# A transformer layer's second output projection in seven products of quarters, with sums made by accumulating transfers

## The chip, the core and the metric

The kernel runs on one core of a Trainium2 chip. A core has five engines with a queue each, which work in order and wait for one another through semaphores: TensorE (PE in the profile; PEld is its weight load), VectorE (DVE), ScalarE (ACT), GpSimd (POOL) and SyncE (SP). Transfers between on-chip memory and the large memory (DRAM) are issued from the queues of SP, ACT or POOL. The metric is the time of one execution on the device, in microseconds; lower is better. The time before is 1794.62 us, the median of three runs from 1794.32 to 1796.17.

## The reference

One decoder layer for 1024 tokens of width 1024, in float32. The part around the change:

```python
y_a = _sliding_window_attention(qa, ka, va, sinks) @ w_oa          # first output projection
y_b = _gated_deltanet(dq, dk, dv, z, b_raw, a_raw, ...) @ w_ob     # second output projection
mixed = (jax.nn.sigmoid(g_a) * y_a + jax.nn.sigmoid(g_b) * y_b) @ w_out
x = _layer_norm(ALPHA * x + (1.0 + gt1) * mixed, ln1_g, ln1_b)
```

Before it stand the input projection `u @ w_in`, which gives queries, keys, values, the gates `g_a`, `g_b` and the inputs of the DeltaNet heads, the attention itself and the recurrence of the eight heads. After it comes a squared-ReLU MLP of width 4096 and a second layer norm. `w_oa`, `w_ob` and `w_out` are 1024 x 1024.

## The kernel before

Activations are kept with the features on the 128 partitions and the tokens along the row. Every matmul operand is split into a high part, rounded by ScalarE (`A.activation` with a copy), and a low part, the rest, by VectorE (`split_s`, L206). A product of a 128x128 block of weights with 512 tokens is then three matmuls of 128x128 by 128x512: high by high, high by low, low by high (L248, L1608). 1024 features by 1024 features by 1024 tokens, done plainly, are 8 output blocks x 8 blocks of the sum x 2 halves of the tokens x 3 = 384 matmuls.

A product of two matrices, cut into quarters, can also be had from seven products of quarters (or of sums of quarters) instead of eight, with more additions. Before the change the first output projection (L1591 to L1619) and the MLP are done so: 7 products x 4 output pairs x 12 matmuls (4 blocks of the sum x 3) = 336 matmuls. The second output projection is plain: eight units of `stream_unit` (L238, L1635) with 48 matmuls each.

Order of work. The program for PE, VectorE and ScalarE is written out in order (`manual_schedule`). A counter, `count[0]`, goes up by one with every large matmul, and `at(p, f, ...)` (L189) puts the work of `f` in front of the matmul with number p. These positions decide an order and not a time: an engine still runs each instruction as soon as its operands are there, and waits in its queue if they aren't. SP and POOL get their transfers in an order that a scheduler makes from the same calls. The stages, with the names of their first positions:

- the gates, queries and keys of the attention, beside the attention of 64 slots of 16 positions (`slot(s)`, L954) and a triangular solve on VectorE. POOL adds score blocks here (`join`, L876) and masks probabilities (`mask`, L915)
- from `Q0`: the heads' inputs, beside the recurrence of the eight heads, 120 positions each (`PER`, L1002; head h begins at R0 + 120 h). Each step of the recurrence goes through PE, VectorE and ScalarE in turn (`hd_a`, `hd_b`, `hd_c`, L1265 to L1304). Extra work of VectorE and ScalarE is placed into free windows of this chain (`window`, L1006). At a head's end `hd_out` (L1330) turns its output, half of the tokens at a time, multiplies it by its gate in the tile `sz` (L1338) and stores `sz` to `og_d` (L1343, on POOL; L1341 for head 7, on SP). `sz` has one buffer: the next head's gate is loaded into it (L1170) when the store has read it
- from `OA`: the first output projection. Quarters `11`, `T2`, `T3`, `T4` of the attention's output are sums that VectorE makes on chip (`ts_step`, L1401; `q_part`, L1430); `21`, `T1`, `22` are loaded from DRAM into tiles `or` (`q_load`, L1421) and split (`q_split`). The sums of the weights are made by VectorE (`o_sum`, L1457). Four accumulators per output block are read while TensorE goes on: `o_part` (L1562, ScalarE) copies an accumulator into a tile `t` or `t0`, and the next product adds to the same accumulator 12 positions later; `o_full` (L1567, VectorE) adds a second accumulator to that tile and stores the block to `ta_d`
- position OA + 336: the second output projection, whose operands `og_load`/`og_split` (L1503) bring in from `og_d`. Its outputs are multiplied by the sigmoid of `g_b`, and `y_a` times the sigmoid of `g_a` is added (`y_load`, `yb_done`, L1574 to L1633), then split for the next stage
- from `E0`: the product with `w_out`, then the MLP

On-chip memory is handed from stage to stage in pools. At position OA + 26 (`CLOSE`, L1500) the heads' pools `pc` and `pce` end, and `big2` and `p2` (tiles `or` and `t`) are opened in the same memory (`open_p2`, L1514). `yo` (tiles `t0`) lives on.

Of the kernel before, what the change touches and what calls it, by code (L numbers as in the profile page):

```python
# [34 lines left out]
def hybrid_layer_kernel(ctx: ExitStack, tc: tile.TileContext,  # L35
# [39 lines left out]
    og_d = dram.tile([KT, P, S], F32, name="og_d")  # L75
# [76 lines left out]
    later = [in_cols(w_ob, f * P) for f in range(KT)]  # L152
# [816 lines left out]

    makers = {"g": gate_done, "k": k_done, "q": q_done}  # L970
# [359 lines left out]
    def hd_out(h, half):  # L1330
# [6 lines left out]
        def put():  # L1337
            V.scalar_tensor_tensor(out=d["sz"][:, halves[half]], in0=tp, scalar=normw, in1=d["sz"][:, halves[half]],  # L1338
                                   op0=ALU.mult, op1=ALU.mult)
            if h == 7:  # L1340
                nc.sync.dma_start(out=og_d[h, :, halves[half]], in_=d["sz"][:, halves[half]])  # L1341
            elif half == 1:
                nc.gpsimd.dma_start(out=og_d[h], in_=d["sz"])  # L1343
# [49 lines left out]
    def ts_load(k):  # L1393
        tags = (((pce, "qT", 3), (pce, "qT", 3)), ((pc, "Re", 1), (pce, "pad", 1)), ((pc, "kT", 2), (pc, "kd", 2)),
                ((pc, "E", 2), (pc, "vr", 2)))[k]
# [5 lines left out]
    def ts_step(k, n):  # L1401
        (r11, r12), (r21, r22) = [[t[:, halves[u]] for u in range(2)] for t in late[k]]
        sub(V, *((r12, r12, r11), (r22, r22, r12), (r21, r21, r22), (r12, r22, r11))[n])
# [37 lines left out]
    wraw, wop, opn = {}, {}, [0]  # L1441

    def o_load(i, pair):
        for j in range(2):
            t = (wp.tile([P, KT, P], F32, tag="wr", name="owr", bufs=2) if pair % 2 == 0 else
                 gpool.tile([P, S], F32, tag="gate", name="owg").rearrange("p (k c) -> p k c", k=KT))
            nc.sync.dma_start(out=t, in_=in_cols(w_oa, (pair + 4 * j) * P)[0])
            wraw[pair, j] = t[:, 0:4, :], t[:, 4:8, :]

    def o_op(i, which):  # L1450
        (f1l, f1h), (f2l, f2h) = wraw[i, 0], wraw[i, 1]
        src = {"a0": f1l, "a4": f1h, "g0": f1l, "g4": f1h, "b0": f2l, "b4": f2h, "d": f2h}[which]
        t = wop[i, which] = wp.tile([P, 2, 4, P], F32R, tag=("wh", "wl")[opn[0] % 2], name="wo")
        opn[0] += 1
        split_s(t[:, 0], t[:, 1], src, 5)

    def o_sum(i, what):  # L1457
        (f1l, f1h), (f2l, f2h) = wraw[i, 0], wraw[i, 1]
        if what == "b":
            add_(V, f2l, f2l, f2h)  # L1460
        elif what == "g0":
            sub(V, f1l, f2l, f1l)
        elif what == "g4":
            sub(V, f1h, f1h, f1l)
        elif what == "G4":
            add_(V, f1h, f1h, f1l)
            sub(V, f1h, f1h, f2l)
        else:
            sub(V, f2h, f2h, f1l)

    at(L0 - 56, o_load, 0, 0)
    at(L0 - 50, o_load, 0, 1)
    OPS = [(-76, 0, "a0"), (-70, 1, "a0"), (-64, 0, "+b"), (-61, 0, "+g0"), (-58, 1, "+b"), (-55, 1, "+g0"),
# [7 lines left out]
    for p, i, what in OPS:  # L1481
        at(OA + p, *((o_sum, i, what[1:]) if what[0] == "+" else (o_op, i, what)))
    for pair in (2, 3):
        at(OA + 97, o_load, 1, pair)

    REST = [(n, j) for n in ("21", "T1", "22") for j in range(2)]
    RSPLIT = (54, 60, 66, 86, 104, 112)

# [12 lines left out]
    oh, ol, ograw = [None] * KT, [None] * KT, {}  # L1501

    def og_load(k):  # L1503
        ograw[k] = p2.tile([P, S], F32, tag="or", name="or", bufs=3)
        nc.sync.dma_start(out=ograw[k], in_=og_d[k])

    def og_split(k):
        oh[k] = big2.tile([P, S], F32R, tag=f"h{k}", name=f"oh{k}")
        ol[k] = big2.tile([P, S], F32R, tag=f"l{k}", name=f"ol{k}")
        for half in range(2):  # L1510
            s_ = halves[half]
            after(4 * half, split_s, oh[k][:, s_], ol[k][:, s_], ograw[k][:, s_])
# [16 lines left out]
    OGK = (6, 7, 0, 1, 2, 3, 4, 5)  # L1529
    OGS = (180, 188, 208, 216, 224, 232, 246, 256)  # L1530
    for n, k in enumerate(OGK):
        at(OA + (150, 152, 154)[n] if n < 3 else OA + OGS[n - 3] + 6, og_load, k)
        at(OA + OGS[n], og_split, k)

# [10 lines left out]
    at(OA + 250, lambda: (wseq.extend(later), w_more()))  # L1545
    for p in (270, 291):
        at(OA + p, w_go)
        at(OA + p + 8, w_more)
# [10 lines left out]
    def o_put(i, c):  # L1559
        nc.gpsimd.dma_start(out=ta_d[i + 4 * (c // 2), :, halves[c % 2]], in_=ot[i, c])  # L1560

    def o_part(i, c, pt, last=False):  # L1562
        A.activation(out=o_tile(i, c), in_=pt, func=AF.Copy)
        if last:
            o_put(i, c)
# [779 lines left out]
```

## Time and profile before

The profile shows one execution. The chip's own time of that execution was 1793.83 us; its span from the first instruction to the last is 1792.1 us, so 1.7 us lie outside the span. It is 0.8 us below the median of the three runs.

| what | value |
|---|---|
| median of three runs | 1794.62 us (1794.32 to 1796.17) |
| profiled execution, its own time | 1793.83 us |
| its span | 1792.1 us |
| granted TensorE clock, mean | 0.999 |
| first output projection, first to last matmul start | 913.1 to 989.6 us |
| second output projection, the same | 989.8 to 1076.7 us |
| bytes moved by transfers | 350.32 MB |

How to read it: the page gives each engine's busy time and its share of the span. Matmuls are pipelined, so the duration in a matmul's row is longer than the distance to the next one's start, and a busy PE isn't PE at its peak. A row of a timeline begins with the start and the duration in us; what stands in square brackets is how long the engine was idle before it and who released it. A row of the waits reads: who waited, for whom, us in total, times, longest. Weights and other tiles go by the program's names (`or`, `t`, `sz`, `qh`), and L1563 is a line of the kernel.

### The profile page before, as it was taken

To read this page: it belongs to the slowest core of one execution; us is meant where nothing else is said; L and a number is where in the kernel's file an instruction comes from. 1 tells how busy PE (TensorE), PEld (TensorE's weight loads), DVE (VectorE), ACT (ScalarE), POOL (GpSimd) and SP (SyncE) were. 2 spreads that over 40 slices of the span, in tenths; PEclk is the share of its full clock that TensorE was granted. 3 is DMA by queue.
4 is the path that set the end of the run, shared out by engine and by line. 5 is a ranking of instruction groups with operands and counts; after the bars stand their busy time and mean duration, and the time that the engine had idled before them with its cause. 6 is when DMAs were issued, how large, how long until landed. Compare 5 with 4: busy or idle time off the path is not lost.

```text
span 1792.1 us, 26317 instructions
## 1 busy us (share of the span) xinstructions
PE 1778.8 (99%) x9134; PEld 1499.3 (84%) x9134; DVE 1305.3 (73%) x2411; ACT 1034.0 (58%) x2363; POOL 326.8 (18%) x478
## 2 busy tenths in 40 slices
PE   9999999999999999999999999999999999999998
PEld 6988888888888888888888888888888888888887
DVE  7689588888855576766687555888777766676697
ACT  4789578887874565655575432475555545434341
POOL 0334234544331011110002200002122210000000
PEclk9999999999999999999999999999999999999999
DMA  9656722232256566665657634369888889665671
GB/s 331 184 198 217 206 80 90 70 104 74 74 210 198 152 173 177 174 189 173 231 161 269 209 124 165 129 193 325 301 276 270 284 294 383 239 200 181 207 258 47
DMA packets 254295, 350.32 MB, mean 195 GB/s; under 512 B 26345, under 2 KB 158130, under 8 KB 253906
## 3 DMA queue, kind: packets, MB, share of 16 engines
q1 hardware_dynamic: 212146, 220.78, 38.5%
q0 software_dynamic: 31488, 106.85, 17.6%
q10 hardware_dynamic: 10528, 21.00, 3.2%
q8 instruction: 72, 1.18, 0.3%
q14 instruction: 61, 0.50, 0.1%
HBM read 238.74 MB, written 107.75 MB: 193 GB/s over the span
## 4 chain that ended last, share of the span: by engine, by line
PE 92%; DVE 3%; ACT 2%; DMA 1%; issue 0%; ACTq 0%; SPq 0%; DVEq 0%
PE mm L250 36%; PE mm L2206 8%; PE mm L2266 7%; PE a L2266 4%; PE b L2206 4%; PE b L2266 4%; PE a L2206 3%; PE mm L1611 2%; PE c L2266 2%; PE c L933 2%; PE mm L1835 1%; PE b L1611 1%; PE mm L178 1%; PE mm L180 1%; PE mm L179 1%; PE a L859 1%
## 5 line engine op out<-in xcount | busy, mean ns | idle before, releaser
L250 PE MATMUL mm<-uh,wh 128*128 128x512 f32 x800 | 319.6, 400 | 0.0
L250 PE MATMUL mm<-uh,wl 128*128 128x512 f32 x800 | 319.3, 399 | 0.0
L250 PE MATMUL mm<-ul,wh 128*128 128x512 f32 x800 | 318.8, 398 | 0.0
L208 DVE TENSOR_TENSOR sp<-sraw,sp 128x1024 fp32r<-128x1024 f32 x112 | 132.8, 1219 | 75.7 <-ACT sp L207 75.6
L207 ACT ACTIVATE sp<-sraw 128x1024 fp32r<-128x1024 f32 x112 | 112.7, 1053 | 120.7 <-PE b L2266 75.4
L250 PEld LDWEIGHTS mm<-uh,wh 128*128 128x128 f32 x800 | 150.7, 188 | 26.2
L250 PEld LDWEIGHTS mm<-ul,wh 128*128 128x128 f32 x800 | 150.8, 188 | 26.1
L250 PEld LDWEIGHTS mm<-uh,wl 128*128 128x128 f32 x800 | 150.8, 188 | 26.1
L2266 PE MATMUL mm<-sp 128*128 128x512 f32 x528 | 135.9, 389 | 0.0
L2266 PEld LDWEIGHTS mm<-sp 128*128 128x128 f32 x528 | 98.8, 188 | 20.3
L2266 PE MATMUL a<-sp 128*128 128x512 f32 x336 | 92.3, 389 | 0.0
L1282 ACT ACTIVATE vn<-a,brk 128x128 f32<-128x128 f32 x64 | 23.6, 369 | 111.0 <-PE a L1280 111.0
L866 DVE CUSTOM_DVE_ANT_0 nscore<-a,amask,nsink 128x256 f32<-128x256 f32 (+1 forms) x128 | 54.4, 462 | 44.3 <-PE a L859 44.1
L2266 PE MATMUL b<-sp 128*128 128x512 f32 (+1 forms) x336 | 79.7, 374 | 0.0
L877 POOL TENSOR_TENSOR sm<-sm 128x256 f32<-128x256 f32 x56 | 58.1, 1038 | 109.6 <-ACT sm L873 81.7
L225 DVE TENSOR_TENSOR wl<-wr,wh 128x1024 fp32r<-128x1024 f32 x56 | 72.6, 1297 | 7.0 <-ACT wh L221 6.7
L2266 PEld LDWEIGHTS a<-sp 128*128 128x128 f32 x336 | 63.1, 188 | 13.1
L2266 PEld LDWEIGHTS b<-sp 128*128 128x128 f32 x336 | 60.3, 188 | 11.2
L208 DVE TENSOR_TENSOR wl<-fraw,wh 128x1024 fp32r<-128x1024 f32 x43 | 52.5, 1221 | 16.5 <-ACT wh L207 16.5
L207 ACT ACTIVATE wh<-fraw 128x1024 fp32r<-128x1024 f32 x43 | 45.0, 1056 | 32.0 <-PE b L2206 27.0
L873 ACT ACTIVATE sm<-nscore,stat 128x257 f32<-128x257 f32 (+1 forms) x128 | 62.0, 487 | 0.4 <-DVE stat L866 0.2
L221 ACT ACTIVATE wh<-wr 128x1024 fp32r<-128x1024 f32 x56 | 59.0, 1054 | 0.7 <-PE mm L179 0.7
(567 smaller groups left out, 4733.4 us busy)
## 6 DMA issues: line engine op xcount, KB each, us to landing
wr<-in_w_in_dram SPq DMA_DIRECT2D x60, 512.0 KB, 3.6
sraw<-hf_d SPq DMA_DIRECT2D x54, 512.0 KB, 4.1
adaw<-in_w_ada_dram SPq DMA_DIRECT2D x83, 256.0 KB, 5.1
fraw<-in_w_ff_dram SPq DMA_DIRECT2D x32, 512.0 KB, 5.4
sraw<-wt_d SPq DMA_DIRECT2D x32, 512.0 KB, 4.3
hf_d<-t ACTq DMA_DIRECT2D x48, 256.0 KB, 4.6
wt_d<-wx POOLq DMA_DIRECT2D x48, 256.0 KB, 3.1
sraw<-in_w_ff_dram SPq DMA_DIRECT2D x22, 512.0 KB, 5.5
```

The source lines that it names most:

```text
L207: A.activation(out=hi, in_=src, func=AF.Copy)
L208: after(lag, lambda: V.tensor_tensor(out=lo, in0=src, in1=hi.bitcast(F32), op=ALU.subtract))
L221: A.activation(out=hl[0], in_=raw, func=AF.Copy)
L225: V.tensor_tensor(out=hl[1], in0=raw, in1=hl[0].bitcast(F32), op=ALU.subtract)
L250: T.matmul(ts[half], lhsT=w[:, k, :], rhs=xx[k][:, sl], start=k == 0 and m == 0, stop=k == KT - 1 and m == 2)
L866: V.tensor_tensor_reduce(out=ns[:, i, 1:1 + W], in0=sc[:, i * 2 * P:i * 2 * P + W], in1=amask[:, mo:mo + W], scale=-1.0, scalar=nsink[:, 2 ...
L873: A.activation(out=sm[:, i, 0:1 + W], in_=ns[:, i, 0:1 + W], func=AF.Exp, scale=-1.0, bias=st[:, i:i + 1], accum_out=st[:, 2 + i:3 + i])
L877: G.tensor_tensor(out=sm[:, :, 1 + P:1 + 2 * P], in0=sm[:, :, 1:1 + P], in1=sm[:, :, 1 + P:1 + 2 * P], op=ALU.add)
L933: T.matmul(av[:, 0:256], lhsT=vt[:, b, :], rhs=p_[:, m, :], start=p_ is full and m == 0, stop=p_ is prods[-1][1] and m == 1)
L1611: T.matmul(pt, lhsT=t[:, lw, k, :], rhs=r[:, k % 2, :], start=begin and k == 0 and x_ == 0, stop=k == 3 and x_ == 2, skip_group_check=True)
L2206: T.matmul(pt, lhsT=a[:, kk, :], rhs=b[k], start=begin and k == 0 and x_ == 0, stop=k == 3 and x_ == 2, skip_group_check=True)
L2266: T.matmul(to, lhsT=a[:, f, t * P:(t + 1) * P], rhs=b[:, f, lo:up], start=(begin or own) and s % NS == 0 and f == 0 and x_ == 0, stop=s % ...
```

## The change

The second output projection is also made of seven products of quarters, 336 matmuls; both projections now run through one loop over `(stage, i, m)`, with pairs of output blocks sharing a weight tile of 128 x 4 x 256. What that needs:

- The sums of quarters of both weight matrices are made in DRAM (`ws_d`) during the attention stage: 16 plain copies of 512 KB from SP (`ws_put`) and 28 transfers of 512 KB from POOL that add to what is there (`ws_add`, `accum_op`). The sums on VectorE (`o_sum`) go.
- Each head's output is stored as seven quarters (`oq_d`): some parts are stored plainly by SP, the others are added by POOL's accumulating transfers of 256 KB; where an output enters with a minus, ScalarE first writes its negative into the head's tile `vr` (for head 7 at 16 positions after the output, else 4). `og_d` goes. `ts_step` makes its sums with the opposite sign, and the fourth pair of its tiles lies elsewhere, since `vr` is now in use.
- The second stage loads 14 pairs of quarters (`q2_load`) and 28 weight blocks serve both stages. Gates are loaded in pairs and applied as blocks become complete (`o_gate`, `y_out`), and the splits for the next stage are placed by hand (`m_split`).

```diff
-    og_d = dram.tile([KT, P, S], F32, name="og_d")
+    oq_d = {name: dram.tile([KT // 2, P, HALF], F32, name=f"oq{name}_d")
+            for name in ("11", "21", "22", "T1", "T2", "T3", "T4")}
+    ws_d = [dram.tile([4, 2, P, 4, 2 * P], F32, name=f"ws{n}_d") for n in "ab"]
...
+    def ws_put(n, q, fk, g):
+        nc.sync.dma_start(out=ws_d[n][q, g], in_=w_block(n, fk, g))
+
+    def ws_add(n, q, fk, g):
+        nc.gpsimd.dma_start(out=ws_d[n][q, g], in_=w_block(n, fk, g), accum_op=ALU.add)
+
+    puts = [(n, q, fk, g) for n in range(2) for q, fk in enumerate(("21", "21", "11", "12")) for g in range(2)]
+    adds = [(n, q, fk, g) for n in range(2) for q, fk in
+            ((0, "22"), (1, "22"), (2, "21"), (3, "11"), (1, "11"), (3, "21"), (3, "22")) for g in range(2)]
+    for i, v in enumerate(puts):
+        at(20 + 24 * i, ws_put, *v)
+    for i, v in enumerate(adds):
+        at(slot(14 + (7 * i) // 4) + 20, ws_add, *v)
...
-            if h == 7:
-                nc.sync.dma_start(out=og_d[h, :, halves[half]], in_=d["sz"][:, halves[half]])
-            elif half == 1:
-                nc.gpsimd.dma_start(out=og_d[h], in_=d["sz"])
+            r, k, o = d["sz"][:, halves[half]], h % 4, oq_d
+            neg = d["vr"][:, halves[half]]
+
+            def more():
+                A.activation(out=neg, in_=r, func=AF.Copy, scale=-1.0)
+                if h < 4 and half == 0:
+                    nc.sync.dma_start(out=o["T2"][k], in_=neg)
+                elif h < 4:
+                    nc.sync.dma_start(out=o["T3"][k], in_=neg)
+                    for name, src in (("T2", r), ("T1", neg), ("T4", neg)):
+                        nc.gpsimd.dma_start(out=o[name][k], in_=src, accum_op=ALU.add)
+                elif half == 0:
+                    nc.gpsimd.dma_start(out=o["T4"][k], in_=neg, accum_op=ALU.add)
+                else:
+                    for name, src in (("T3", r), ("T4", r), ("T2", neg)):
+                        nc.gpsimd.dma_start(out=o[name][k], in_=src, accum_op=ALU.add)
+
+            for name in ((("11", "T1", "T4") if half == 0 else ()) if h < 4 else (("21", "22")[half],)):
+                nc.sync.dma_start(out=o[name][k], in_=r)
+            act(16 if h == 7 else 4, 2.7, more)
...
+    BCT, TUR = (2, 5, 3), (1, 6, 7, 4)
+    CHAINS = [[(0, m), (1, m)] for m in TUR], [(0, 2), (0, 5), (1, 2), (1, 5), (0, 3), (1, 3)]
+    for stage, g, first in ((0, 0, 0), (0, 1, 1), (1, 0, 1), (1, 1, 0)):
...
+    wsplit = [-76, -52, -15, 2] + [endof[ops[n - 4]] + 2 for n in range(4, len(ops))]
+    for n, p in enumerate(wsplit):
+        at(OA + p, w_split, n)
+        at(OA + ((-104, -102)[n] if n < 2 else wsplit[n - 2] + 7), w_load, n)
...
+    ORDER2 = ("11", "21", "T1", "22", "T2", "T3", "T4")
+    REST2 = [(n, j) for n in ORDER2 for j in range(2)]
+    RSPLIT2 = (150, 160, 242, 250, 260, 270, 290, 306, 350, 362, 386, 398, 422, 440)
...
+    def y_out(i, c, src):
+        y = sgt[i + 4 * (c // 2)][:, halves[c % 2]]
+        V.tensor_tensor(out=y, in0=src, in1=y, op=ALU.mult)
+        V.tensor_tensor(out=y, in0=y, in1=gates_[1, i // 2, c][:, i % 2], op=ALU.add)
...
-    for f in range(KT):
-        stream_unit(oh, ol, yb_done(f))
```

More of the change, by code (lines that the diff above doesn't have):

```diff
@@ L151, in hybrid_layer_kernel @@
         wseq.append(in_cols(w_in, {"q": C_DQ, "v": C_DV, "g": C_GB}[kind] + i * P))
-    later = [in_cols(w_ob, f * P) for f in range(KT)]
+    later = []
     for q in (0, 1, 0):
@@ L1439, in hybrid_layer_kernel @@
             at(OA + ps_[k], q_part, name, k)
[L1441 to L1473, printed above, removed]
[7 rows of a table removed]
@@ new lines, in hybrid_layer_kernel, with w_load, w_split @@
+    for n, (stage, i, m) in enumerate(turns):
+        endof[stage, i // 2, m] = 12 * (n + 1)
+    wraw, wop = {}, {}
+    def w_load(n):
+        stage, g, m = ops[n]
+        kind, v = WHICH[m]
+        wraw[n] = wp.tile([P, 4, 2 * P], F32, tag="wr", name="owr", bufs=2)
+        nc.sync.dma_start(out=wraw[n], in_=w_block(stage, v, g) if kind == "A" else ws_d[stage][v, g])
+    def w_split(n):
+        hi, lo = wop[ops[n]] = [wp.tile([P, 4, 2 * P], F32R, tag=tag, name="wo") for tag in ("wh", "wl")]
+        split_s(hi, lo, wraw[n], 5)
@@ L1500, in hybrid_layer_kernel, with q2_load, q2_split @@
     CLOSE = OA + 26
[L1501 to L1512, printed above, removed]
+    quad2 = {}
+    def q2_load(name, j):
+        qraw[name, j] = t = p2.tile([P, 2, HALF], F32, tag="or", name="or", bufs=3)
+        nc.sync.dma_start(out=t, in_=oq_d[name][2 * j:2 * j + 2].rearrange("k p c -> p k c"))
+    def q2_split(name, j):
+        pool, i = HOME2[name]
+        quad2[name, j] = [(big, big2)[pool].tile([P, 2, HALF], F32R, tag=f"{c}{i + j}", name="q" + c) for c in "hl"]
+        split_s(*quad2[name, j], qraw[name, j], 5)
     def open_p2():
@@ L1557, in o_tile, with pair_rows, ga_load @@
         return ot[i, c]
-    def o_put(i, c):
-        nc.gpsimd.dma_start(out=ta_d[i + 4 * (c // 2), :, halves[c % 2]], in_=ot[i, c])
-    def o_part(i, c, pt, last=False):
+    gates_ = {}
+    def pair_rows(d, i, c):
+        f = 2 * (i // 2) + 4 * (c // 2)
+        return d[f:f + 2, :, halves[c % 2]].rearrange("f p c -> p f c")
+    def ga_load(g, c):
+        gates_[0, g, c] = t = gpool.tile([P, 2, HALF], F32, tag="gate", name="ga")
+        nc.gpsimd.dma_start(out=t, in_=pair_rows(ga_d, 2 * g, c))
+        after(22, lambda: A.activation(out=t, in_=t, func=AF.Sigmoid))
@@ L1563, in o_part, with ta_load, o_gate @@
+    def ta_load(g, c):
+        gates_[1, g, c] = t = gpool.tile([P, 2, HALF], F32, tag="gate", name="ta")
+        nc.gpsimd.dma_start(out=t, in_=pair_rows(ta_d, 2 * g, c))
+    def o_part(i, c, pt):
         A.activation(out=o_tile(i, c), in_=pt, func=AF.Copy)
-        if last:
-            o_put(i, c)
+    def o_gate(i, c, src):
+        t = ot[i, c] if (i, c) in ot else o_tile(i, c)
+        V.tensor_tensor(out=t, in0=src or t, in1=gates_[0, i // 2, c][:, i % 2], op=ALU.mult)
+        nc.gpsimd.dma_start(out=ta_d[i + 4 * (c // 2), :, halves[c % 2]], in_=t)
@@ new lines, in m_split @@
+    def m_split(f, half):
+        if mh[f] is None:
+            mh[f] = big.tile([P, S], F32R, tag=f"h{f}", name="mh")
+            ml[f] = big.tile([P, S], F32R, tag=f"l{f}", name="ml")
+        sl = slice(0, S) if half is None else halves[half]
+        hi, lo, y = mh[f][:, sl], ml[f][:, sl], sgt[f][:, sl]
+        if f < 4:
+            split_s(hi, lo, y)
+            return
+        A.activation(out=hi, in_=y, func=AF.Copy, scale=-1.0)
+        after(6, lambda: V.scalar_tensor_tensor(out=lo, in0=y, scalar=-1.0, in1=hi.bitcast(F32),
+                                                op0=ALU.mult, op1=ALU.subtract))
@@ L1605, in hybrid_layer_kernel @@
         pt = obank[i, ab]
+        own = slice((i % 2) * P, (i % 2 + 1) * P)
         for k in range(4):
```

128 lines of the change are left out of this document (67 added, 61 removed), and 7 rows, old and new, of the table OPS.

## The prediction

> **What bounds the kernel now.** I read the page first, then the waits by engine, then the stretch of the two output projections. These are the page's first line, its engine line, its DMA rates over 40 slices, and the shares of the chain that ended last.
>
> ```profile
> span 1792.1 us, 26317 instructions
> PE 1778.8 (99%) x9134; PEld 1499.3 (84%) x9134; DVE 1305.3 (73%) x2411; ACT 1034.0 (58%) x2363; POOL 326.8 (18%) x478
> GB/s 331 184 198 217 206 80 90 70 104 74 74 210 198 152 173 177 174 189 173 231 161 269 209 124 165 129 193 325 301 276 270 284 294 383 239 200 181 207 258 47
> PE 92%; DVE 3%; ACT 2%; DMA 1%; issue 0%; ACTq 0%; SPq 0%; DVEq 0%
> ```
>
> TensorE is busy throughout and makes 92% of the chain. The view of its own waits says the same: two start-up waits and then almost nothing.
>
> ```profile
> PE b L115 <- DMA rows_a<-in_b_ada_dram: 2.2, 1, 2.2
> PE warm L308 <- DVE zer L623: 1.8, 1, 1.8
> PE b L1706 <- ACT rawu L1709: 0.2, 1, 0.2
> ```
>
> So a matmul taken away is time won, as long as nothing else makes TensorE wait. What is one worth? Its row says 389 ns, but matmuls overlap, so the price is the distance between starts. One group of the first projection, and the first and last groups of the second (name, count, ns, first and last start):
>
> ```profile
> L1611 PE MATMUL mm<-qh,wo x128: 389/389/458, 913.1 to 989.6; 128*128 128x512 f32 x128
> ...
> L250 PE MATMUL mm<-oh,wh x128: 389/389/389, 989.8 to 1076.2; 128*128 128x512 f32 x128
> L250 PE MATMUL mm<-oh,wl x128: 389/389/389, 990.3 to 1076.7; 128*128 128x512 f32 x128
> ```
>
> The second projection's 384 matmuls start between 989.8 and 1076.7 us: 86.9 / 383 = 0.227 us each. A position of the kernel's planning counter, one matmul, is therefore 0.227 us here.
>
> **Removed.** Seven products of quarters for four output pairs are 7 x 4 x 12 = 336 matmuls in place of 384: 48 x 0.227 = 10.9 us off the path. The weights' sums on VectorE (18 operations of 128x512) and the products of the first gate move or go too. That is worth nothing by itself, since VectorE and ScalarE have room in these stretches (windows: heads' weights and attention, heads, first projection, second; length, then busy us of PE, PEld, DVE, ACT, POOL, clock, DMA share, GB/s):
>
> ```profile
> 200.00:540.00 340.00, 340.00 (x1797) 292.35 (x1796) 271.13 (x646) 262.49 (x819) 141.90 (x171) 1.00 0.35 108
> 540.00:913.00 373.00, 373.00 (x2331) 322.58 (x2330) 247.97 (x571) 213.02 (x631) 34.02 (x56) 1.00 0.59 176
> 913.00:990.00 77.00, 77.00 (x343) 63.61 (x342) 56.24 (x83) 43.94 (x72) 11.89 (x22) 1.00 0.76 255
> 990.00:1077.00 87.00, 87.00 (x386) 72.03 (x385) 48.58 (x69) 33.34 (x41) 13.96 (x26) 1.00 0.51 161
> ```
>
> **Added in the attention stretch.** 16 stores on SP and 28 accumulating transfers on POOL, each 512 KB. They are last needed about 1,100 positions later, so their own time is hidden. Their bytes (44 x 0.52 MB, and 28 x 0.52 MB read back) are 38 MB in 340 us, 111 GB/s on top of 108: less than the 255 GB/s at which the first projection still runs. On POOL an issue costs what one costs now:
>
> ```profile
> L950 POOL DMA_DIRECT2D attn_d<-at x32: 539/557/1437, 239.8 to 534.1; - x32
> ```
>
> 28 x 0.56 = 16 us on an engine busy for 142 of 340. Queued behind an issue are the attention's masks and joins. The issue is planned right behind a join, and a mask has 19 positions (4.3 us) before TensorE reads it, so I cost it at nothing; without that cover it would be up to 16 us.
>
> **Added for the heads.** 16 negations on ScalarE (128x512, about 0.6 us each, 10 us beside 213 of 373), 28 accumulating transfers of 256 KB on POOL, and stores on SP. For the first six heads the buffers they hold are wanted again some 40 positions later: hidden. Two places are not.
>
> **The last head and the handover of the pool.** The tiles of the first projection's pools (`or`, `t`) lie in memory that the heads' pool gives back at position OA+26. Here is who made SP wait for its first load into them, then the DVE, SP and ACT instructions around it:
>
> ```profile
> SPq L1425 <- DVE ql L208: 7.3, 4, 3.1
> SPq L1425 <- DMA gb_d<-gz: 2.6, 1, 2.6
> SPq L1425 <- DMA og_d<-sz: 1.2, 2, 0.6
> ```
> ```profile
> 913.57 1.40 DVE L1338 SCALAR_TENSOR_TENSOR sz<-b,convc,sz 128x512 f32<-128x512 f32 x2
> 917.28 0.62 ACT L207 ACTIVATE qh<-ts 128x512 fp32r<-128x512 f32 x1
> 922.11 0.68 DVE L208 TENSOR_TENSOR ql<-ts,qh 128x512 fp32r<-128x512 f32 x1
> 922.86 0.89 SPq L1425 DMA_DIRECT2D or<-attn_d  x2
> 922.87 0.60 ACT L1563 ACTIVATE t<-mm 128x512 f32<-128x512 f32 x1 [1.15 <-PE mm L1611]
> 926.94 1.06 ACT L207 ACTIVATE qh<-or 128x1024 fp32r<-128x1024 f32 x1 [1.15 <-DMA or<-attn_d]
> 929.24 0.58 ACT L1563 ACTIVATE t<-mm 128x512 f32<-128x512 f32 x1
> ```
>
> SP's load and ACT's first write of a `t` start within 0.01 us of each other, right after VectorE's last read of the old pool ended (922.11 + 0.68). The pool is handed over as a whole: its last user, a store of another tile too, releases everybody. And it is on the path. TensorE's product 7 for the first pair begins at position 48 (913.1 + 48 x 0.227 = 924.0) and adds to the bank that ACT copies at 922.87 to 923.47; product 4 begins at position 72, 929.4, on a bank copied at 929.24 to 929.82, behind two splits that waited for SP's loads. The second link has no slack:
>
> ```profile
> PEld mm L1611 <- ACT t L1563: 0.2, 1, 0.2
> ```
>
> So TensorE loses what the handover loses. In the change the last head's transfers become users of that pool. The negation stands at position 15, behind the split of 917.28, and is done near 918.3. Then `T4 += -r` is issued, and `T4 += r` of the other half must wait until that has landed. With a for one accumulating transfer of 256 KB, from issue to a released waiter, the pool is free at 918.3 + 2a, against 922.86 now: 2a - 4.6 us lost.
>
> No accumulating transfer is in this trace. The nearest rows: POOL's plain 256 KB stores at line 2036 (landing, min/median/max), its plain 512 KB stores, and one of these with the load that waited for it:
>
> ```profile
> DMA to landing us min/median/max: 2.2/3.2/9.0
> og_d<-sz POOLq DMA_DIRECT2D x7, 512.0 KB, 3.7
> 890.15 0.54 POOL L1343 DMA_DIRECT2D og_d<-sz  x1 [38.72 <-DMA gb_d<-gz]
> 895.01 0.53 POOL L1170 DMA_DIRECT2D sz<-z_d  x1 [4.33 <-DMA og_d<-sz]
> ```
>
> 895.01 - 890.15 = 4.86 against a landing of 3.7: a waiter sees the end 1.16 us late. A plain store of 256 KB is then 2.2 + 1.16 = 3.4 at best and 3.2 + 1.16 = 4.4 in the middle. The low end is the best one; an accumulating transfer that ended sooner than a plain one is excluded, since it reads its target as well. The high end is two middling ones in a row, 8.7. I take 5.0, close to the middling plain store: 4.36 plus a second pass of 262,144 bytes at the page's best slice (383 GB/s, 0.68 us), since the queues are quiet there (below). Lost: 2 x 5.0 - 4.6 = 5.4 us (2.2 at a = 3.4, 12.8 at 8.7).
>
> [...]
>
> **Head 6's buffer.** `sz` is single: head 7's load waits until head 6's is read. This is already tight, as ACT's wait shows, with the little idle time behind it; the two DVE rows are head 6's outputs:
>
> ```profile
> 882.07 0.74 DVE L1338 SCALAR_TENSOR_TENSOR sz<-b,convc,sz 128x512 f32<-128x512 f32 x1
> 889.11 0.74 DVE L1338 SCALAR_TENSOR_TENSOR sz<-b,convc,sz 128x512 f32<-128x512 f32 x1
> 899.63 0.63 ACT L1174 ACTIVATE sz<-sz 128x512 f32<-128x512 f32 x1 [0.49 <-DMA sz<-z_d]
> 902.62 0.63 ACT L207 ACTIVATE qh<-ts 128x512 fp32r<-128x512 f32 x1 [1.06 <-PE mm L250]
> ```
>
> The first accumulation follows the first output (882.8) and its negation, 0.6 us and some 1.2 us of ACT's queue: 884.6. The second can start after the second output and one issue, 889.85 + 0.56 = 890.4, and after the first has landed, so it lands at max(890.4, 884.6 + a) + a. The load of today starts at 895.0. At a = 5.0 it starts 0.4 us later, which the 1.06 us of idle time covers: nothing. Above a = 5.8 it costs 884.6 + 2a - 895.0 - 1.06 = 2a - 11.5.
>
> **The second projection's new shape.** It copies and adds out of banks that TensorE goes on using 12 positions (2.7 us) later. Its operations by today's durations:
>
> ```profile
> L1631 DVE TENSOR_TENSOR sg<-sg,ta 128x512 f32<-128x512 f32 x16 | 11.1, 692 | 0.5
> L208 DVE TENSOR_TENSOR ql<-or,qh 128x1024 fp32r<-128x1024 f32 x6 | 7.3, 1224 | 4.4 <-ACT qh L207 4.3
> ```
>
> The densest stretch is the 48 positions (10.9 us) of products 1, 6, 7, 4 of the first two pairs: 12 VectorE operations of 0.69 and 3 of 1.22 are 11.9 us. A queue of 1 to 2 us fits into 2.7 less 0.69, barely. I take 0.5 us of waits (0 to 3).
>
> **Sum.** -10.9 + 5.4 + 0.5 = -5.0 us. The profiled execution took 1793.83 us (1.7 of it outside the span), 0.8 below the median of the runs, 1794.62. So 1788.8 for it and 1789.6 for the median. 0.2% (3.6 us) is about what a measurement of this kernel can tell from no change.
>
> **Rivals.** Full gain: two transfers as fast as the fastest plain store, 2.2 us each with nothing behind the landing, would free the pool at 918.3 + 4.4 = 922.7, no later than VectorE frees it now, and TensorE gains the whole 10.9 us: 1783.7. For it speaks that the DMA engines stand nearly still when these transfers would run (rates between 913 and 930 us, slices of 0.43 us):
>
> ```profile
> GB/s 0 0 0 0 0 337 381 405 357 352 371 198 48 24 24 29 0 0 0 0 0 0 0 0 0 34 63 313 361 178 308 410 429 347 342 332 382 355 348 349
> ```
>
> Against it speaks the 4.86 us above; chance 0.17. [...]
>
> Slower: the serial accumulations decide. Above a = 5.8 both places pay, -10.9 + (2a - 4.6) + (2a - 11.5) + 0.5, which is zero at a = 6.6. At 8.7 it is +8.3, 1802.9. For it: every such transfer reads its target first, and the two on `T4` cannot overlap. Against it: the transfers are small and the queues quiet. Chance 0.20, half of it within 0.2%.
>
> VectorE's queue in the second projection: 16 handovers after 12 positions, and if 6 of them wait 1 us, the sum is -10.9 + 5.4 + 6 = +0.5, 1795.1. For it: 11.9 us of work in 10.9; against: the stretch before it has room to run ahead, and back to back the operations start closer than they last. Chance 0.10. Attention's masks pushed late by POOL's issues: some 0.1 us at 28 places would turn -5.0 into -2.2, 1792.4; against it speaks the cover of 4.3 us; chance 0.05.
>
> **The numbers.** The forecast, with a between 3.4 and 6.6, keeps 0.48; it alone runs from 1786.4 to 1794.6. Faster by over 0.2% needs a below 5.7: most of the forecast and all of the full gain, 0.60. Within: 0.22. Slower: 0.18. The range reaches to the full gain and half-way into the slow case: 1784.0 to 1798.0.
>
> **What would show it.** 336 matmuls between the first and last start of each projection; SP's first load of `or` behind an accumulation, at about 15 us after the first projection's first matmul instead of 9.8; a wait of TensorE for ACT's copy of `t` near positions 48 and 72, of some 5 us together, that is not there now; ACT's wait for head 7's `sz` hardly longer. I am wrong if a lies far from 5, if the handover does not wait for these transfers, or if TensorE waits in another stretch.

## The result: slower by 74 us, and where the time went

The changed kernel takes 1868.39 us (median of four runs, 1863.9 to 1872.29), against 1794.57 us for the kernel before (median of four, 1794.32 to 1796.17). The ratio is 1.0409, with a 95% interval from 1.0382 to 1.0435. The forecast was 1789.6 us with a range up to 1798.0. The profiled execution took 1870.48 us.

First the page of the changed kernel, in the lines that answer to those shown of before. The two rows in the middle are slices of a fortieth of the span: the granted TensorE clock in tenths, and the share of time in which the DMA engines were busy.

```profile
span 1868.8 us, 26423 instructions
PE 1785.4 (96%) x9085; PEld 1499.5 (80%) x9086; DVE 1314.1 (70%) x2391; ACT 1055.9 (57%) x2374; POOL 376.4 (20%) x519
...
PEclk9887999999999999999999999999999999999999
DMA  9998992223226568876768875357988779865671
...
PE 75%; DMA 9%; DVE 5%; ACT 5%; issue 5%; POOL 1%; SPq 0%; ACTq 0%; POOLq 0%; DVEq 0%
```

TensorE made 92% of the chain before and makes 75% now, and the DMA engines are full in the first slices, where the clock falls too. Where the time went is read from four first starts of matmuls: of the gates, of the first projection, of the product with `w_out`, and the end. Before (the first projection's 913.1 stands in the prediction), then after:

```profile
L250 PE MATMUL mm<-uh,wh x800: 387/392/499, 164.7 to 912.3; 128*128 128x512 f32 x160
...
L1835 PE MATMUL mm<-wh,mh x64: 388/389/477, 1076.9 to 1162.2; 128*128 128x512 f32 x64
```
```profile
L252 PE MATMUL mm<-uh,wh x800: 387/392/632, 224.1 to 977.4; 128*128 128x512 f32 x160
...
L1671 PE MATMUL mm<-qh,wo x256: 387/389/795, 978.2 to 1135.1; 128*128 128x512 f32 x128
...
L1887 PE MATMUL mm<-wh,mh x64: 388/389/477, 1152.5 to 1237.8; 128*128 128x512 f32 x64
```

| stretch | before | after | difference |
|---|---|---|---|
| start to the gates' first matmul | 164.7 | 224.1 | +59.4 |
| from there to the first projection (attention and heads) | 748.4 | 754.1 | +5.7 |
| the two projections | 163.8 | 174.3 | +10.5 (forecast: -5.0) |
| the rest | 715.2 | 716.3 | +1.1 |

So most of the loss lies ahead of everything that the change was written into. What runs there now? These are the instructions of line 981, the additions to the weights' sums, then what GpSimd waited for ahead of them, and their time to landing:

```profile
L981 POOL DMA_DIRECT2D wsa_d<-in_w_oa_dram x14: 1129/1144/1667, 49.1 to 124.8; - x14
L981 POOL DMA_DIRECT2D wsb_d<-in_w_ob_dram x14: 1144/1211/1748, 116.2 to 261.2; - x14
...
  DMA wsa_d<-in_w_oa_dram: 86.3, 8
  DMA wsb_d<-in_w_ob_dram: 22.3, 5
...
DMA to landing us min/median/max: 6.4/10.0/14.9
```

They were planned into the attention (whose masks began at 231.9 us before) and run from 49.1 to 261.2 us. `at` fixes the order on TensorE, VectorE and ScalarE alone; the transfers of SP and GpSimd wait for nothing there, so the scheduler put them where these queues looked free. An issue takes 1.14 to 1.21 us in the middle, and GpSimd stands 108.6 us in its queue until an earlier copy or addition to the same target has landed. 46.4 of these lie ahead of the first addition at 49.1 us, where the kernel before has no work for GpSimd either (its next starts at 61.8 us); 62.2 us are left that can delay something. What that does to TensorE shows in the waits up to 260 us:

```profile
DVE mt L715 <- POOL e L651: 35.6, 2, 31.3
...
PE a L640 <- DVE mt L715: 30.0, 1, 30.0
...
PE mm L561 <- ACT ba L583: 13.0, 1, 13.0
```

`e` of line 651 is a mask that GpSimd makes for the triangular solve. It stood behind the additions (the first one starts at 158.0 us, 100.6 before), VectorE behind it, and TensorE behind VectorE for 30 us. The windows (length, then busy us of PE, PEld, DVE, ACT, POOL, clock, DMA share, GB/s) say the same of the DMA engines, before and after:

```profile
0.00:110.00 110.00, 105.70 (x633) 87.58 (x634) 80.31 (x166) 71.40 (x148) 21.29 (x32) 1.00 0.75 241
110.00:165.00 55.00, 55.00 (x293) 46.73 (x292) 49.84 (x118) 50.82 (x118) 25.90 (x34) 1.00 0.65 218
```
```profile
0.00:110.00 110.00, 86.64 (x495) 72.20 (x497) 59.18 (x111) 50.27 (x86) 23.74 (x31) 0.92 1.07 283
110.00:165.00 55.00, 23.87 (x123) 18.82 (x122) 19.45 (x52) 22.31 (x66) 19.09 (x21) 0.73 1.12 247
```

Three quarters busy before, full after (a share of 1 or a little above is read as full): the start had little room for the 23 MB that these transfers write.

**The handover.** The last head's four accumulating transfers on GpSimd, the first load and the first copy into the new pool (timelines by engine, merged):

```profile
982.38 0.84 POOL L1376 DMA_DIRECT2D oqT_d<-sz  x1 [19.77 <-DVE ql L210]
984.49 0.85 POOL L1373 DMA_DIRECT2D oqT_d<-vr  x1 [1.27 <-ACT vr L1365]
985.53 0.84 POOL L1376 DMA_DIRECT2D oqT_d<-vr  x1 [0.18 <-issue]
991.17 0.84 POOL L1376 DMA_DIRECT2D oqT_d<-sz  x1 [4.81 <-DMA oqT_d<-vr]
995.83 0.89 SPq L1466 DMA_DIRECT2D or<-attn_d  x2
995.97 1.09 ACT L1604 ACTIVATE t<-mm 128x512 f32<-128x512 f32 x2 [8.26 <-issue]
```

`T4 += -r` goes out at 984.49; `T4 += r` waits for it and goes out at 991.17; the pool is free at 995.83, which is 17.6 us after the first matmul. The two links are 6.7 and 4.7 us long. TensorE's waits in the projections, and what follows the longest of them:

```profile
PE mm L1671 <- ACT t L1604: 6.8, 1, 6.8
...
PE mm L1671 <- DVE t L1426: 4.4, 4, 1.6
...
PE b L1671 <- ACT t L1604: 2.9, 1, 2.9
...
PE b L1671 <- DVE t L1426: 0.6, 1, 0.6
```
```profile
996.62 0.80 PE L1671 MATMUL mm<-qh,wo 128*128 128x512 f32 x1 [6.79 <-ACT t L1604]
997.21 0.63 PE L1671 MATMUL mm<-ql,wo 128*128 128x512 f32 x1
997.63 1.05 PE L1671 MATMUL mm<-qh,wo 128*128 128x512 f32 x2
998.49 0.63 PE L1671 MATMUL mm<-ql,wo 128*128 128x512 f32 x1
...
1002.41 0.62 PE L1671 MATMUL mm<-qh,wo 128*128 128x512 f32 x2
1002.87 0.39 PE L1671 MATMUL mm<-ql,wo 128*128 128x512 f32 x1
...
1041.46 1.06 ACT L1597 ACTIVATE ga<-ga 128x1024 f32<-128x1024 f32 x1 [5.11 <-DMA ga<-ga_d]
...
1043.05 0.79 PE L1671 MATMUL b<-qh,wo 128*128 128x512 f32 x1 [2.85 <-ACT t L1604]
```

The waits are 14.7 us. All 672 matmuls are in the trace, so each wait can be given its position: the one of 6.79 us stands at 48, and those of 2.85, 0.65 and 1.65 us (228, 288 and 324) still lie in the first projection. In the second one, from position 336 on, only 2.7 us are lost (at 432, 456 and 660). The last two rows show the second longest wait: ScalarE stands for a gate's load, with the copy of a block behind it.

After the wait of 6.79 us three matmuls take 1.28 us (997.21 to 998.49), 0.43 each, until about 1001.9, and only then 0.23 again. So a wait costs more than itself: 672 matmuls of 0.227 us are 152.5 us, the waits make 167.2, and the stretch took 174.3. Of the other 7.1 us, 4.3 are matmuls at a lower granted clock (0.50 from 996.62 to 1001.90 us, 0.54 from 1043.0 to 1046.6): 13 distances in the 5.56 us behind this wait and 8 in the 3.47 us behind the one of 2.85 us, in place of 0.227 us each. The rest are single distances a little above 0.227, many of them beside the waits.

### The profile page after: what moved, and what is told of

It reads as the page before. It is cut to its first block, busy times and chain, and to the rows that moved or that the text cites. A ratio compares the mean times of both kernels' runs of the same rounds, so it can differ in the third digit from the quotient of the medians.

```text
span 1868.8 us, 26423 instructions
## 1 busy us (share of the span) xinstructions
PE 1785.4 (96%) x9085; PEld 1499.5 (80%) x9086; DVE 1314.1 (70%) x2391; ACT 1055.9 (57%) x2374; POOL 376.4 (20%) x519
## 4 chain that ended last, share of the span: by engine, by line
PE 75%; DMA 9%; DVE 5%; ACT 5%; issue 5%; POOL 1%; SPq 0%; ACTq 0%; POOLq 0%; DVEq 0%
PE mm L252 26%; PE mm L2258 7%; PE mm L2318 6%; PE a L2318 4%; PE b L2318 4%; PE b L2258 4%; PE a L2258 2%; PE mm L1671 2%; PE c L2318 2%; DMA v_d<-vs 2%; PE c L935 2%; DMA wsb_d<-in_w_ob_dram 1%; PE mm L1887 1%; DMA wsa_d<-in_w_oa_dram 1%; DMA ga<-ga_d 1%
## 5 line engine op out<-in xcount | busy, mean ns | idle before, releaser
L1671 PE MATMUL mm<-qh,wo 128*128 128x512 f32 x256 | 83.2, 401 | 11.3 <-ACT t L1604 6.8
L868 DVE CUSTOM_DVE_ANT_0 nscore<-a,amask,nsink 128x256 f32<-128x256 f32 (+1 forms) x128 | 54.3, 462 | 39.6 <-PE a L861 39.3
L1671 PEld LDWEIGHTS mm<-qh,wo 128*128 128x128 f32 x256 | 49.3, 192 | 24.7 <-ACT t L1604 7.4
L227 DVE TENSOR_TENSOR wl<-wr,wh 128x1024 fp32r<-128x1024 f32 x48 | 62.9, 1310 | 6.9 <-ACT wh L223 6.7
L210 DVE TENSOR_TENSOR wo<-owr,wo 128x1024 fp32r<-128x1024 f32 x28 | 34.2, 1222 | 42.3 <-ACT wo L209 42.3
```

Source lines behind the costliest of these rows:

```text
L210: after(lag, lambda: V.tensor_tensor(out=lo, in0=src, in1=hi.bitcast(F32), op=ALU.subtract))
L227: V.tensor_tensor(out=hl[1], in0=raw, in1=hl[0].bitcast(F32), op=ALU.subtract)
L868: V.tensor_tensor_reduce(out=ns[:, i, 1:1 + W], in0=sc[:, i * 2 * P:i * 2 * P + W], in1=amask[:, mo:mo + W], scale=-1.0, scalar=nsink[:, 2 ...
L1671: T.matmul(pt, lhsT=lw[:, k, own], rhs=r[:, k % 2, :], start=begin and k == 0 and x_ == 0, stop=k == 3 and x_ == 2, skip_group_check=True)
```

## The experiments

The theory after the result: the weights' sums cost the time by where their transfers stand, and the last head's accumulations by holding the pool. The rivals: the transfers cost what they cost anywhere (bytes on the DMA engines, issues on GpSimd); the pool is late for another reason. The kernel before ran at 1796.44 us beside the first four, 1795.96 beside the next two, then 1797.9, 1796.04, 1795.44 and 1796.29 beside the later pairs and single runs. Times with one run each are single executions. Ten executions of the mended kernel at the end lie between 1795.75 and 1801.62 us, so a difference of a few us between two single ones isn't shown by the times; such a reading rests on the waits in the traces.

**No sums.**

```diff
-        at(20 + 24 * i, ws_put, *v)
...
-        at(slot(14 + (7 * i) // 4) + 20, ws_add, *v)
...
+        in_=w_block(stage, v if kind == "A" else ("22", "22", "21", "11")[v], g)
```

> Leaves out all transfers that make the weights' sums; the four sums are read as plain quarters of the weights. Theory: the 59.4 us lost ahead of the gates' first matmul (164.7 to 224.1) come from these transfers alone, since the scheduler put them at the start of the kernel; first gates matmul back at 165 +- 2, and most of the 5.7 us lost between there and the first projection goes too: 1803 to 1809 us. The 10.5 us that the two projections grew by (163.8 to 174.3) stay. Rival, the start is late for another cause of the new order: above 1840.

Measured: 1809.67 us, gates' first matmul at 166.0, first projection at 916.0. The theory holds, with the time 0.7 us above its range: 58.1 us of the start and 4.1 us of the attention came from these transfers. The projections stay long (176.0 us), so two separate losses have to be explained.

**Copies from ScalarE's queue.** ScalarE's queue follows the written order, and an addition can't be issued ahead of the copy under it.

```diff
-        nc.sync.dma_start(out=ws_d[n][q, g], in_=w_block(n, fk, g))
+        nc.scalar.dma_start(out=ws_d[n][q, g], in_=w_block(n, fk, g))
...
+            at(p - 40, ws_put, *u)
+        at(p, ws_add, *v)
```

> Computes the same; the 16 plain copies of the weights go from ScalarE's queue, which follows the written order, 40 positions ahead of the first addition to the same target, so that SP's and GpSimd's share can't be moved to the start. Theory, the place costs and not the transfers: as without the sums, 1803 to 1811 us, first gates matmul at 165 +- 2. Rival, 28 issues of 1.14 us on GpSimd and 23 MB beside the attention cost what they cost wherever they stand: masks and joins late by 1 us at 28 places, above 1830 us.

Measured: 1849.89 us. The start is right (166.0), but 40 us are lost in the attention instead, so the theory as stated fell: the place alone isn't it. What GpSimd waited for ahead of the additions, and TensorE's first two waits:

```profile
  DMA wsb_d<-in_w_ob_dram: 36.8, 7
  DMA wsa_d<-in_w_oa_dram: 35.7, 9
```
```profile
PE c L935 <- POOL pl L920: 21.6, 7, 6.3
PE b L903 <- ACT sm L887: 7.1, 7, 2.4
```

GpSimd stands 72.5 us for landings, the masks (`pl`) and joins stand behind it, and TensorE waits for both. The scheduler had again chosen the order within GpSimd's queue: where two additions go to one target, it often put the second right behind the first, so it had to wait until that one landed, 6.8 us in the middle (51.4 of the 72.5 us; the rest is for copies). Bytes and issues were not ruled out yet; a later run does that.

**Additions to targets of their own, and small additions.** Both read plain quarters in place of the sums, so that only the transfers' cost is seen.

```diff
-        nc.gpsimd.dma_start(out=ws_d[n][q, g], in_=w_block(n, fk, g), accum_op=ALU.add)
+        nc.gpsimd.dma_start(out=wx_d.pop(), in_=w_block(n, fk, g), accum_op=ALU.add)
```

> The weights' sums are not used (plain quarters are read instead), and each of the 28 accumulating transfers goes to a target of its own, so that GpSimd's queue never stands waiting for a copy or an earlier addition; the bytes and the place at the start stay. Theory, GpSimd's queue stands still (86.3 + 22.3 us of waits, with the attention's first parts queued behind): at most 25 of the 59.4 us stay, below 1838 us. Rival, the bytes: 165 us at a DMA share of 0.72 and 23 MB more at 283 GB/s (82 us) need 201 us, so at least 36 us stay, 1845 us or more.

```diff
-        nc.gpsimd.dma_start(out=ws_d[n][q, g], in_=w_block(n, fk, g), accum_op=ALU.add)
+        nc.gpsimd.dma_start(out=ws_d[n][q, g, 0:16], in_=w_block(n, fk, g)[0:16], accum_op=ALU.add)
```

> The weights' sums are not used (plain quarters are read instead); the order, the waits and the count of the 44 transfers stay, but each accumulating transfer moves 16 of the 128 rows, 64 KB. Theory, GpSimd's queue stands still: it still waits for the 16 copies (62.3 + 22.3 us of waits), so at least 45 of the 59.4 us stay, above 1853 us. Rival, the bytes: 10 MB at 283 GB/s (36 us) fit beside a share of 0.72 in 165 us, so at most 15 us stay, below 1825 us.

Measured: 1889.39 us with targets of their own (the gates begin at 247.0), 1817.45 us with small additions (at 175.4, 9.4 later than without any). Both numbers are the rival's, but neither run changed the bytes or the standing alone. With small additions the order of GpSimd's queue is the same and five sixths of the loss are gone. GpSimd still stands 73.9 us, but 46.2 of these lie ahead of its first addition, and behind it the standing fell from 62.2 to 27.7 us. With targets of their own the additions wait for no copy, so they moved: they run from 1.4 to 96.0 us in place of 49.1 to 261.2. There TensorE waits for loads, not for GpSimd:

```profile
PE b L401 <- DMA xin<-in_x_dram: 22.9, 8, 7.1
PE a L352 <- DMA adaw<-in_w_ada_dram: 16.7, 8, 5.5
```

SP issues these loads, GpSimd the additions; the DMA engines are full there (a share of 1.15 over the first 110 us), and TensorE's waits for these loads, 39.6 us together, are not there in the kernel before. Nor did GpSimd's standing go in this run: in 19 waits, 61.7 us together, one of its transfers still waited until an earlier one had landed (a landing took 34.7 us in the middle). How the change's own 59.4 us divide between full engines and GpSimd's standing therefore stays open. Small additions shorten both.

**Additions spaced out.** The same 44 transfers, bytes and stage as with the copies from ScalarE's queue; the order on GpSimd differs, and the copies stand 20 positions earlier.

```diff
+            pmask[0] = G.affine_select(out=flat4(part), in_=flat4(full), ...
...
+        with tc.issue_after(pmask[0].ins):
+            nc.gpsimd.dma_start(out=ws_d[n][q, g], in_=w_block(n, fk, g), accum_op=ALU.add)
...
+            at(p - 60, ws_put, *u)
```

> Computes the same as the change. The 16 copies go from ScalarE's queue 60 positions ahead of the first addition to their target, and each of the 28 additions is held behind the last mask issued on GpSimd at its planned slot, so that two additions to one target never stand back to back. Bytes, count and stage are those of the run before it with the copies on ScalarE (1849.9 us), which stood 72 us in GpSimd's queue for landings. Theory, standing in GpSimd's queue made its loss in the attention: GpSimd's waits for these transfers fall under 10 us, TensorE's waits for the masks (21.6 us) go, and the time is that without any sums (1809.7) plus 0 to 6: 1810 to 1816 us. Rival, the bytes and the 28 issues of 1.15 us make it: 1840 us or more.

Measured: 1812.01 us, as the theory said, and GpSimd doesn't wait for these transfers once. The same window of the attention without sums, with the copies on ScalarE's queue, and spaced:

```profile
270.00:380.00 110.00, 110.00 (x593) 95.06 (x592) 94.54 (x221) 90.86 (x291) 56.53 (x62) 1.00 0.28 84
```
```profile
270.00:380.00 110.00, 95.30 (x483) 80.32 (x482) 80.57 (x181) 74.33 (x236) 56.47 (x63) 0.95 0.83 168
```
```profile
270.00:380.00 110.00, 110.00 (x593) 95.03 (x593) 96.36 (x220) 91.34 (x290) 65.57 (x74) 1.00 0.80 174
```

593 matmuls without the transfers and 593 with all of them, at a DMA share of 0.80 in place of 0.28. The product with `w_out` starts at 1092.3 us, against 1092.0 without any sums. In the attention the bytes and the issues are hidden, and standing in GpSimd's queue is the whole loss.

**The last head by way of DRAM.** Its output and negative are stored plainly, and GpSimd adds from there.

```diff
+                    if h == 7:
+                        nc.sync.dma_start(out=on_d[:, half], in_=neg)
+                        if half == 1:
+                            nc.sync.dma_start(out=on_d[:, 2], in_=r)
+                        n_, r_ = on_d[:, half], on_d[:, 2]
```

> As the run with the additions spaced out, and the last head stores its output and its negative plainly into DRAM, from where GpSimd adds them to the quarters, so that no accumulating transfer reads the pool that is handed over. Theory, two accumulations in a row hold the pool and stop TensorE (waits of 6.4 and 2.2 us for ScalarE's copies without the sums, each followed by some microseconds at half the granted clock): both waits fall to under 2 us together, and the run is 9 to 13 us below the one with the additions alone spaced. Rival, the waits come from the loads into the new pool (the DMA engines are busy 0.67 to 0.9 of the time there), which start as late behind plain stores: less than 4 us below.

Measured: 1806.69 us, 5.3 below the run before it: between the two theories. The pool is handed over 11.8 us after the first matmul (17.0 in the run before it), but the loads into it take 7.5 us (4.1 before the change) beside the additions, and ScalarE's copy stands behind a split that waits for one of them.

**The last head out of the pool, and later sigmoids.**

```diff
+        heads[h]["sz"] = gpool.tile([P, S], F32, tag="gate", name="sz") if h == 7 else big4("sz", bufs=1)
...
+                d["neg"] = gpool.tile([P, S], F32, tag="gate", name="neg")
```

> As the run with the additions spaced out (1812.0 us), but the last head's gate and its negative lie in two tiles of the gates' pool, which lives on, so that none of its transfers, plain or accumulating, reads the pool that is handed over. Theory, the transfers of the last head hold the pool: it is handed over when VectorE has read it, at most 10 us after the first projection's first matmul (17.6 in the change, 11.8 with the plain stores), TensorE's waits for ScalarE's copies near positions 48 and 72 go (6.4 us with the additions spaced, 6.1 with the plain stores), and with them 3 us at half the granted clock: 1798 to 1803 us. Rival, the loads into the new pool are slow for another reason and ScalarE's splits hold the copies anyway: 1805 us or more.

```diff
-        after(22, lambda: A.activation(out=t, in_=t, func=AF.Sigmoid))
+        after({(1, 0): 52, (1, 1): 46, (1, 3): 34, (1, 2): 26}.get((g, c), 22),
```

> As the one before it in this list, and the sigmoids of the gates that the second and third pair of blocks need later (stage 0, the four loads from position 190 on) stand 52, 46, 34 and 26 positions behind their load's position in place of 22. Theory, the wait of 2.3 to 3.2 us for ScalarE's copy out of the second bank comes from ScalarE standing in its queue for the gate's load (4.6 us in the run with the plain stores, landed at 978.7) with that copy behind it: the wait goes, with some 1.8 us at a lower clock after it, 3 to 5 us below the run without this edit. Rival, the copy is late for the bank itself or for VectorE: under 1 us.

Measured: 1806.97 us with the tiles moved (the rival's time), 1803.94 us with the sigmoids later too. The waits near positions 48 and 72 fell to 1.9 us, but the handover came only 11.5 us after the first matmul. In the second run this is what ScalarE's copy then waited for:

```profile
ACT t L1612 <- DMA gb_d<-gz: 2.7, 1, 2.7
```

It is the last of the plain stores of 256 KB that were there before the change. It needs 7.8 us to land in the first run, against 4.4 before, while the DMA engines are nearly full beside it (a share of 0.89 from 916 to 930 us of the second). Both theories had a part: the accumulations hold the pool, and behind them the bytes do. The sigmoids' edit did remove its wait (6.6 us for ScalarE's copy out of the second bank in the first run, none in the second), but the time fell by only 3.0 us: VectorE's waits went from 5.1 to 9.9 us.

**Splits spread, and a later negative.**

```diff
-    RSPLIT2 = (150, 160, 242, 250, 260, 270, 290, 306, 350, 362, 386, 398, 422, 440)
+    RSPLIT2 = (150, 160, 206, 212, 219, 236, 312, 324, 346, 354, 364, 374, 386, 398)
```

> As the run with the sigmoids moved (1803.9 us); the splits of the second projection's operands leave the two dense stretches (positions 240 to 336, and 408 on) for the stretches where VectorE adds no blocks (168 to 240, 336 to 408). Theory, VectorE's queue is what TensorE waits for there: per 24 positions (5.4 us) two additions, two gates, one split of weights and 1.5 splits of operands are 5.8 us; without the last 4.0 us. Of the 9.9 us of waits for VectorE's blocks at most 5 stay: 1796 to 1800 us. Rival, VectorE is late because the weights' loads are (one landed 9 us after its issue, with ScalarE waiting 3.7 us for it): less than 2 us below.

```diff
-            act(16 if h == 7 else 4, 2.7, more)
+            act(36 if h == 7 else 4, 2.7, more)
```

> As the one before it in this list, and the last head's negative is made 20 positions later, so that its accumulations (and the first gates' loads behind them) move out of the stretch in which the pool is handed over. Theory, the handover still waits for a plain store of a gate unit (landing 7.8 us, DMA engines 0.9 busy) which the accumulations and weights' loads slow down: handover 1 to 3 us earlier, 1 to 4 us below the run without this edit. Rival, the weights' loads alone fill the DMA engines: within 1 us, or slower where the gates now come late.

This run also moves the first pairs' gates back: two sigmoids to 60 positions behind their load, and four products with gates to positions 130 to 145.

Measured: 1805.75 and 1804.3 us. The first is a miss: VectorE's dense stretch was thinned out, and TensorE waits as long, since ScalarE now stands for an operand's load with the copies of blocks behind it. From the second run, ScalarE and then TensorE:

```profile
1010.55 1.06 ACT L209 ACTIVATE qh<-or 128x1024 fp32r<-128x1024 f32 x1 [3.29 <-DMA or<-oqT_d]
...
1017.07 1.06 ACT L209 ACTIVATE qh<-or 128x1024 fp32r<-128x1024 f32 x1 [4.02 <-DMA or<-oqT_d]
1018.03 0.58 ACT L1612 ACTIVATE t<-b 128x512 f32<-128x512 f32 x1
```
```profile
1018.66 0.79 PE L1679 MATMUL b<-qh,wo 128*128 128x512 f32 x1 [3.88 <-ACT t L1612]
```

The later negative brought the handover from 11.7 to 11.1 us, less than expected; the 1.4 us between the two times are too few to tell.

**Mended, and mended again.** The operands' loads get 45 positions or more, and all transfers of the last head go behind the negative; then loads that crowd are moved later.

```diff
+    RSPLIT2 = (150, 160, 206, 212, 224, 252, 262, 276, 340, 346, 356, 386, 394, 404)
...
+                if h == 7:
+                    A.dma_start(out=o[("21", "22")[half]][k], in_=r)
```

> As the run with the later negative (1804.3 us); the last head's plain stores and its third accumulation follow the negative too, and the loads of the second projection's operands are placed so that each has at least 45 positions (10 us) from its issue to its split (27 to 41 for those that came late). Theory, what is left of TensorE's waits (9.3 us) is ScalarE standing in its queue for operands' loads that need 7 to 8 us to land while the DMA engines are 0.85 to 1.04 busy, with copies of blocks behind them: the waits of 3.9 and 2.5 us go, and with them some 4 us at half the granted clock; the handover comes 2 us earlier: 1792 to 1797 us, about as the kernel before. Rival, the loads are late whatever their place, since the DMA engines are full: above 1801 us.

```diff
+    RLOAD2 = [RSPLIT[n + 3] + 1 for n in range(3)] + [151, 161, 226, 236, 248] + [RSPLIT2[n - 3] + 1 for n in range(8, 14)]
...
+    for p, q, f in ((30, 72, 0), (36, 78, 1), (42, 90, 4), (48, 100, 5), ...
```

> As the run before it (1799.6 us, 1.0023 of the kernel before); loads that crowd in two stretches where the DMA engines are 0.93 to 1.00 busy are issued later (three operands' loads by 19 to 23 positions, two gates' by 14 to 16, four of the second gate's by 28 to 40), so that the weights' loads between them land sooner. Theory, what is left is ScalarE waiting for one weights' load (3.8 us, landed 9.1 us after its issue) and one operand's (2.4 us) in these stretches, and TensorE behind it (1.9 and 2.3 us, each with some 2 us at half the granted clock): 1792 to 1796 us, a ratio of 0.998 to 1.000. Rival, the transfers' total is too much for these stretches and the waits only move: 1798 us or more, a ratio of 1.002 or more.

Measured: 1799.63 us, ratio 1.0023 [1.0013, 1.0033], and 1798.96 us, ratio 1.0014 [1.0005, 1.0023]. In the first the handover comes 8.0 us after the first matmul (915.4), earlier than before the change (9.8), the last plain store, issued at 919.0, has landed by then, and the waits at it are gone:

```profile
923.36 0.88 SPq L1476 DMA_DIRECT2D or<-attn_d  x2
```

The theory was right on the handover and missed its time by 2.6 us. The second run's time is the rival's, though its ratio is not quite: two waits of 0.6 and 0.7 us went and another grew (from 2.30 to 4.05 us), so the waits only move.

```profile
1023.12 0.80 PE L1683 MATMUL mm<-qh,wo 128*128 128x512 f32 x1 [4.05 <-DVE t L1436]
```

No version tried here beats the kernel before. In the mended kernel the two projections take 164.8 us, against 163.8 before and 152.5 for 672 matmuls without a wait: 6.7 us are TensorE's waits, and the other 5.6 matmuls further apart than 0.227 us. Its profiled span is 5.6 us longer than that of the kernel before, and only 1.0 of these lies in the projections; 2.3 lie ahead of them and 2.3 behind, and no run here tells why. Between 930 and 1010 us its DMA engines are 0.93 to 1.06 busy (0.76 in the first projection before).

## Why the prediction was wrong, point by point

- **The price of a matmul** was right: 48 fewer, 0.227 us apart wherever the clock is full.
- **"Added in the attention stretch ... their own time is hidden" is the step that failed**, and with it 62 of the 77 us that the profiled span grew by. The step took the planned positions for the place where the transfers run. The section on the kernel before says that SP and GpSimd get their order from a scheduler; the step was worked out as if they didn't. No rival covered that either. Its second gap was the queue: it counted 28 issues (at 0.56 us each, read from plain stores of 128 KB; measured 1.14 to 1.21) and asked what a late issue delays, but not that an addition waits in GpSimd's queue for the one before it. The runs showed both: 58 us at the start without a held order, 40 us in the attention with the place right and the queue standing, and with neither 0.3 us up to the product with `w_out` (2.3 between two single times, 1812.0 and 1809.7). What the step said of bytes, and of the masks' 4.3 us of cover, holds in that last run, where TensorE does not wait for a mask once.
- **The heads**: hidden, nearly. That stretch is 1.6 us longer without any sums (750.0 against 748.4).
- **The handover**: mechanism right, size off. Forecast 15.2 us after the first matmul, measured 17.6: the first addition went out 1.1 us later than worked out, and the two links took 6.7 and 4.7 us where 5.0 each was taken. TensorE waited 6.8 us in place of 5.4. Freeing the pool from the accumulations brought the handover to 11.5 us only, since a plain transfer held it next; it came to 8.0 us only when all of the last head's transfers stood behind the negative.
- **Head 6's buffer**: ScalarE's wait for head 7's gate grew to 3.7 us, more than "hardly longer", but TensorE did not wait for it.
- **The second projection's queue** was taken at 0.5 us (0 to 3) and measured 2.7, all for VectorE, inside its range.
- **The first projection's own queues** had no term, though the change put it into the same loop: 5.1 us of waits in it (2.3 for VectorE and 2.85 for ScalarE, beside the handover's). ScalarE's was no rival either: it stands for a load, with copies of blocks behind it (removed by the later sigmoids).
- **What follows a wait** had no term: 7.1 us, 4.3 of them at a granted clock of 0.50 to 0.54. The projections' +10.5 against -5.0 are 1.4 from the handover, 2.2 from the second projection's queue, 5.1 from the first one's and these 7.1, together 15.8, within 0.3 of the difference of 15.5.

## What to carry to other kernels

Before a transfer is called hidden, find out what fixes its place in its queue; one with no dependence goes wherever the scheduler finds the queue free, and it can be held by a dependence or by an explicit order. Transfers that add to the same target should stand at least one landing time apart in their queue (6.8 us in the middle here): back to back they held GpSimd for 51.4 us, and spaced out not once. And a saving of matmuls that is paid for in transfers has to be checked against the DMA share of the very stretch in which they run, and against what a wait of TensorE costs with the clock after it.

## What the runs showed of the hardware

- An accumulating transfer of 512 KB from DRAM to DRAM takes GpSimd 1.14 to 1.21 us to issue in the middle of each group (0.58 for a plain store of 512 KB before). It lands after 6.8 us in the middle in the attention (the copies on ScalarE's queue; 7.7 spaced), and after 10.0 at the start, where the DMA engines are full (a share of 1.07 over the first 110 us). One of 256 KB from on-chip memory lands after 4.0 us at the earliest in the changed kernel, and after 5.7 to 6.6 in the middle (three lines); SP's plain stores of 256 KB there land after 2.1 to 2.9 in the middle.
- After some waits the granted clock of TensorE fell to half: 0.50 from 996.62 to 1001.90 us of the changed kernel, after a wait of 6.79 us, with the matmuls 0.43 us apart. They are 0.43 us apart in the mended kernel too, from 980.43 to 983.42 us, after a wait of 1.94 us. But from 950 to 1000 us of the run with later sigmoids the clock was 1.00, and the matmuls stood 0.23 us apart behind a wait of 3.03 us, so by these runs the length of a wait alone doesn't tell whether the clock falls.
- A DMA share of 0.80 in place of 0.28 in the attention cost TensorE nothing, 593 matmuls in 110 us both times.
